# A transformer layer's feed-forward part: Strassen's seven products over both layers instead of Winograd's form over part of the first

## The chip, the cores and the metric

The kernel runs on one core of a Trainium2 chip. Its engines work side by side, each through its own queue in order: TensorE (PE) multiplies, VectorE (DVE) and ScalarE (ACT) work on tiles in the on-chip memory and on the eight banks in which PE sums, GpSimd (POOL) works on on-chip tiles only and issues some DMAs, and SyncE (SP) issues most of them. The metric is the time of one execution in microseconds (us), as the median of several runs. Tiles have 128 partitions; a size such as 128x320 is partitions by columns.

## What is computed

One layer of a hybrid trunk on 640 tokens of width 1024 (128 context tokens, 512 latent ones), in float32: a modulated RMS norm, an input projection, two attention mixers, a gated merge and output projection, and then the part that the change is about, a feed-forward network of inner width 4096, with a final norm:

```python
x = x + g1 * _merge(a_o, b_o, ga, gb, w_br_a, w_br_b, w_out)
h2 = _rmsnorm(x, n2) * (1 + sc2) + sh2
x = x + g2 * (jnp.square(jax.nn.relu(h2 @ w_mlp_in)) @ w_mlp_out)
y = _rmsnorm(x, final_norm_g)
```

Shift, scale and gate (sh2, sc2, g2 and so on) are products of a conditioning vector with the columns of a 1024 x 6144 matrix, one set for context tokens and one for latent ones.

## The kernel before

Features lie on partitions, tokens on columns, so an activation is eight tiles of 128x640. Every product is made in three passes: each operand is split into a high part of reduced precision (hi) and what is left (lo), and PE sums hi·hi, hi·lo and lo·hi in one bank. The unit of work is one 128-column tile of a weight by one half of the tokens (320): 8 feature tiles deep, 24 matmuls of 128x320 (`gemm_k`, L339 to L341).

A weight tile is loaded (512 KB, SP's queue, tile `wst`), ACT copies its hi part, and DVE or POOL subtracts that to get the lo part (L301, L302); a table names the tiles whose lo part POOL makes. Six tiles of hi and lo parts are there in all, so that the preparation runs three weights ahead. `Weights.conv` does this in the order in which `w_order` lists the weights.

The program goes through the input projection with the first norm, attention with the rest of the projection between its steps, the merge (`AOS` on, L1038 and after), the output projection with the second norm, and the feed-forward part. From the merge on, DVE's instructions stand in the order in which they are written; the other engines' order, and DVE's in other places, is set by a scheduler of the framework. Modulation columns that are needed late are computed on DVE from the merge on (`late_mods`, L992: four multiplies of 128x512 with a running sum for each of 32 tiles of 1024 columns, loaded by POOL's queue as `wmt`), paced by a budget for each product.

The feed-forward part has four chunks of 1024 inner features. For each, the first layer gives eight hidden tiles, relu and square split them into parts (`relu2`), and the second layer multiplies them and adds the gated result to x (`add_gated`, L1100). The first layer of chunk 0 is made plainly, 16 units. In chunks 1 to 3 it takes Winograd's form of a 2x2 product: for each pair of weight tiles, seven products of half the depth and half the tokens (12 matmuls each, L1191 to L1193) instead of eight. The blocks of a weight pair and their sums are prepared in `Weights.block` (sums `sr`, L260, on DVE; hi parts, L280, on ACT; lo parts `wb`, L281, two of seven on POOL); those of the activations are formed once, in `t_pieces`, beside chunk 0. The results are combined on DVE from the banks (L1209). The second layer is plain in all four chunks.

Of the kernel before, what the change touches and what calls it, by code (L numbers as in the profile page):

```python
# [28 lines left out]
WP1 = 4  # L29
# [14 lines left out]
PLAIN = (0,)  # L44
SUMP = ()
BLKP = ('A12', 'A22')
RL = 1
OU = 1800
MG = 2
W2P = 2  # L50
# [7 lines left out]
def trunk_layer(ctx: ExitStack, tc: tile.TileContext, xT, small_in, wmodA, wmodB, tabs, cacheK, cacheV, bias,  # L58
# [10 lines left out]
    pp = ctx.enter_context(tc.tile_pool(name="pp", bufs=1, space=bass.MemoryType.PSUM))  # L69
# [13 lines left out]
    def h_pair(name):  # L83
        return tuple(hp_.tile([P, NT], F32R, tag="h", bufs=16, name=name + x) for x in "hl")

    def o_tile(name, dt=F32):
        return hp_.tile([P, NT], dt, tag="o", bufs=9, name=name)
# [4 lines left out]
    def tt_tile(name):  # L92
        return cur["p"].tile([P, NT], F32R, tag="tt", bufs=12, name=name)
# [16 lines left out]
    def r32(ap):  # L110
        return ap.bitcast(F32)
# [52 lines left out]
    def sq_add(acc, x, f, sl):  # L164
        """sum of squares over the feature tiles but the last, whose squares are returned"""
# [6 lines left out]
    def rstd_half(acc, last, rstd, sl):  # L172
        p, n = ps_t(), sl.stop - sl.start
# [6 lines left out]
    def w_order():  # L180
# [10 lines left out]
        for c in range(4):  # L191
            if c in PLAIN:
                for n in range(KT):
                    yield ("w1", 8 * c + n), w1[8 * c + n]
            else:
                for i in range(8 * c, 8 * c + KT, 2):
                    yield ("A11", i), (w1[i], w1[i + 1])
                    for x in ("A12", "S2", "S3", "A22", "S1", "S4"):
                        yield (x, i), None
            for n in range(KT):  # L200
                yield ("w2", 8 * c + n), w2[c, n]
# [5 lines left out]
    def flush_later(todo=None):  # L207
        todo = later if todo is None else todo
        n = len(todo)
        for f in todo[:n]:  # L210
            f()
# [1160 lines left out]
```

## Time and profile before

| | us |
|---|---|
| runs: 1008.04, 1005.4, 1005.79; median | 1005.79 |
| span of the profiled execution, first to last instruction | 1001.3 |
| merge | 349 to 488 |
| output projection and second norm | 488 to 545 |
| feed-forward part, to its last matmul | 545 to 991 |
| last norm and stores | 991 to 1001 |

The profile is of one execution. Its times count from the span's start, and the runs' times hold some us more than the span. Busy times are of each engine; a group's row gives the line in the kernel, engine, operation, tile written and tiles read, shape and count, then busy time in us and the mean of one instruction in ns, then the engine's idle time just before them and whose work ended it. PE's matmuls are pipelined, so a row of it shows 0.31 us for one matmul, though the next starts earlier.

### The profile page before, as it was taken

Reading aid. Unit: us, or ns where it says so; the run is one execution under the profiler, and the core shown is the slowest. Engines: PE = TensorE matmul, PEld = TensorE weight load, DVE = VectorE, ACT = ScalarE, POOL = GpSimd, SP = SyncE. Lnnn points to the kernel's source line nnn. Section 1 sums busy time; section 2 is a strip of 40 time slices with the busy share of each in tenths; the row PEclk is TensorE's granted clock in tenths of the full one; section 3 lists DMA queues with packets and bytes.
Section 4 is the critical chain, followed back from the end, with each engine's and each line's share of the span. In section 5 each row is a group of like instructions: output and inputs, shape, how many; then the busy total and the mean of one; then the engine's idle time right before and its main releaser. Section 6 shows DMA issues by size and latency. Waiting matters only on the chain.

```text
span 1001.3 us, 16554 instructions
## 1 busy us (share of the span) xinstructions
PE 955.0 (95%) x6317; PEld 908.8 (91%) x6317; DVE 705.0 (70%) x1576; ACT 517.6 (52%) x1117; POOL 173.5 (17%) x154
## 2 busy tenths in 40 slices
PE   7979899999899999999999999999999999999996
PEld 5778778978889999999998899999999999999896
DVE  4479898788866789788587677778733884368644
ACT  5475676668655564654324564237611662156542
POOL 0352232212231011201132100012200220012100
PEclk9999899999999999999999899999999999999999
DMA  9942101312543455556742153212320233120302
GB/s 347 208 172 69 31 25 44 77 43 77 135 111 103 133 160 189 181 169 185 224 126 81 47 164 110 85 43 84 106 78 28 85 106 88 60 79 29 126 22 105
DMA packets 34767, 108.47 MB, mean 108 GB/s; under 512 B 4320, under 2 KB 8032, under 8 KB 34688
## 3 DMA queue, kind: packets, MB, share of 16 engines
q1 hardware_dynamic: 27072, 82.63, 26.5%
q0 software_dynamic: 6464, 23.47, 8.1%
q10 hardware_dynamic: 1152, 1.31, 0.4%
q8 instruction: 49, 0.80, 0.3%
q14 instruction: 30, 0.25, 0.1%
HBM read 99.14 MB, written 4.60 MB: 104 GB/s over the span
## 4 chain that ended last, share of the span: by engine, by line
PE 65%; DVE 15%; ACT 8%; issue 3%; DMA 1%; POOL 0%; ACTq 0%; DVEq 0%; POOLq 0%; SPq 0%
PE pg L339 7%; PE pg L340 7%; PE pg L341 7%; PE pss L340 7%; PE pss L341 7%; PE pss L339 6%; PE pt L339 4%; PE pt L341 4%; PE pt L340 4%; DVE sr L260 3%; ACT wb L280 2%; PE pt L653 1%; PE pt L710 1%; DMA wst<-w 1%; DVE n L641 1%
## 5 line engine op out<-in xcount | busy, mean ns | idle before, releaser
L301 ACT ACTIVATE wh<-wst 128x1024 fp32r<-128x1024 f32 x84 | 88.8, 1057 | 112.4 <-PE pg L340 37.9
L302 DVE TENSOR_TENSOR wl<-wst,wh 128x1024 fp32r<-128x1024 f32 x53 | 64.8, 1223 | 67.5 <-ACT wh L301 67.4
L302 POOL TENSOR_TENSOR wl<-wst,wh 128x1024 fp32r<-128x1024 f32 x31 | 75.1, 2423 | 160.0 <-ACT wh L301 151.5
L992 DVE SCALAR_TENSOR_TENSOR mt<-wmt,cb 128x512 f32<-128x512 f32 x128 | 81.4, 686 | 0.0
L281 POOL TENSOR_TENSOR wb<-wst,wb 128x512 fp32r<-128x512 f32 x24 | 31.7, 1322 | 263.4 <-ACT wb L280 226.6
L339 PE MATMUL pss<-hidh,wh 128*128 128x320 f32 x216 | 67.0, 310 | 0.7 <-ACT hidh L1143 0.7
L340 PE MATMUL pss<-hidl,wh 128*128 128x320 f32 x216 | 67.0, 310 | 0.3
L341 PE MATMUL pss<-hidh,wl 128*128 128x320 f32 x216 | 66.7, 309 | 0.0
L607 DVE TENSOR_TENSOR pl<-pt,ph 128x512 fp32r<-128x512 f32 (+2 forms) x80 | 50.5, 633 | 18.3 <-ACT ph L606 17.3
L606 ACT ACTIVATE ph<-pt 128x512 fp32r<-128x512 f32 (+2 forms) x80 | 44.2, 555 | 28.8 <-PE pt L710 11.7
L280 ACT ACTIVATE wb<-sr 128x512 fp32r<-128x512 f32 x48 | 29.8, 627 | 51.5 <-DVE sr L260 35.6
L1150 DVE TENSOR_TENSOR hidl<-rl,hidh 128x320 fp32r<-128x320 f32 x64 | 37.5, 586 | 25.2 <-ACT hidh L1143 24.6
L988 POOL DMA_DIRECT2D wmt<-wmodB x32 | 17.1, 536 | 174.6 <-DVE mt L992 108.0
L340 PE MATMUL pg<-hidl,wh 128*128 128x320 f32 x144 | 44.7, 310 | 2.2 <-DVE hidl L1150 2.2
L281 DVE TENSOR_TENSOR wb<-sr,wb 128x512 fp32r<-128x512 f32 x48 | 36.0, 755 | 14.2 <-ACT wb L280 14.1
L339 PE MATMUL pg<-hidh,wh 128*128 128x320 f32 x144 | 44.7, 310 | 0.0
L341 PE MATMUL pg<-hidh,wl 128*128 128x320 f32 x144 | 44.5, 309 | 0.0
L340 PE MATMUL pt<-hidl,wh 128*128 128x320 f32 x136 | 42.1, 310 | 1.1 <-DVE hidl L1150 1.1
L341 PE MATMUL pt<-hidh,wl 128*128 128x320 f32 x136 | 42.0, 309 | 0.0
L339 PE MATMUL pt<-hidh,wh 128*128 128x320 f32 x136 | 42.0, 309 | 0.0
L644 ACT ACTIVATE pa<-pss,nm 128x320 f32<-128x320 f32 x64 | 33.1, 522 | 17.2 <-DVE nm L642 17.0
L339 PEld LDWEIGHTS pss<-hidh,wh 128*128 128x128 f32 x216 | 40.5, 188 | 1.5 <-ACT hidh L1143 1.5
(957 smaller groups left out, 3469.9 us busy)
## 6 DMA issues: line engine op xcount, KB each, us to landing
wst<-w SPq DMA_DIRECT2D x64, 512.0 KB, 3.6
wmt<-wmodB POOLq DMA_DIRECT2D x32, 512.0 KB, 4.2
wst<-w_in SPq DMA_DIRECT2D x31, 512.0 KB, 3.6
ms<-wmodA SPq DMA_DIRECT2D x16, 512.0 KB, 8.8
x<-xT SPq DMA_DIRECT2D x16, 320.0 KB, 6.1
bt<-bias SPq DMA_DIRECT2D x16, 320.0 KB, 3.3
wst<-w_br SPq DMA_DIRECT2D x8, 512.0 KB, 4.4
wst<-w_out SPq DMA_DIRECT2D x8, 512.0 KB, 3.5
```

Of the source, the lines that this page charges most:

```text
L280: ACT.activation(t[:, lo4], src, AF.Copy)
L281: later.append(lambda: (nc.gpsimd if name in BLKP else DVE).tensor_sub(t[:, hi4], src, r32(t[:, lo4])))
L301: ACT.activation(hi, st, AF.Copy)
L302: (nc.gpsimd if key in WPOOLSET else DVE).tensor_sub(lo, st, r32(hi))
L339: PE.matmul(ps, wh[:, k], xh[:, sl], start=first, stop=False)
L340: PE.matmul(ps, wh[:, k], xl[:, sl], start=False, stop=False)
L341: PE.matmul(ps, wl[:, k], xh[:, sl], start=False, stop=last)
L606: ACT.activation(ph[:, :n], pt[:, :n], AF.Copy)
L607: DVE.tensor_sub(pl[:, :n], pt[:, :n], r32(ph[:, :n]))
L644: ACT.activation(p[:, HALVES[j]], ps[j][:, :HT], AF.Exp, bias=nm, accum_out=s2[:, j:j + 1])
L992: DVE.scalar_tensor_tensor(t, st[:, q * 512:(q + 1) * 512], 1.0, r32(cb[2 * q + i][:, :512]), op0=OP.mult, op1=OP.mult, accum_out=parts[:, ...
L1150: DVE.tensor_sub(dst[1][:, sl], r[:, :HT], r32(dst[0][:, sl]))
```

## The change

Both layers of the feed-forward part are made by Strassen's form with 7 products of half the depth and half the tokens for each pair of weight tiles, 16 pairs in each layer. The operand blocks are A11 to A22 of a weight pair and B11 to B22 of the activations (feature halves by token halves). Each of the seven products M1 to M7 goes over all the pairs in turn, so that its activation operand is formed and split once (`make_set`, `form`), and its weight operand for each pair. The hidden layer of 4096 features stays on chip in float32 (`HID`), and the second layer sums its depth of four chunks in one bank for each product and pair. The products come in groups: in layer 1 M2 and M4, then M1, M6 and M7, then M3 and M5; in layer 2 M2 and M4, M3 and M5, M1 and M6, and M7.

A weight pair's blocks are loaded again for each group that needs them. POOL forms every sum of weight blocks (L1163) and, for the products in `POOL_LOW`, the lo part (L1180); DVE makes the other lo parts. There are four tiles each for `s` and `s2`, in which sums wait, six for loads, and six for split operands as before. The gates of the feed-forward part (tiles 24 to 31 of the modulation) go from DVE to POOL, with ACT summing (`last_mods`), in the merge. DVE's written order now ends with the output projection; after it the scheduler sets all. The eight banks of the feed-forward part are one pool.

```diff
+POOL_LOW = {(1, "M4"), (2, "M4"), (2, "M3")}
...
+    def last_mods(n):
+        st = dp.tile([P, 1024], F32, tag="ms2", bufs=1, name="wmg")
+        MISC.dma_start(st, wmodB[n])
+        for q in range(2):
+            for i in range(2):
+                t = wp.tile([P, 512], F32, tag="s", bufs=4, name="mg")
+                nc.gpsimd.tensor_mul(t, st[:, q * 512:(q + 1) * 512], cb[2 * q + i])
+                ACT.activation(t, t, AF.Copy, accum_out=parts[:, q, n, i:i + 1])
...
+    def split_set(t, src):
+        ACT.activation(t[:, 0:4], src, AF.Copy)
+        DVE.tensor_sub(t[:, 4:8], src, r32(t[:, 0:4]))
+        return t
+
+    def form(raw, name):
+        a, b, op = {"D4": (B21, B11, OP.subtract), "D3": (B12, B22, OP.subtract), "M1": (B11, B22, OP.add),
+                    "M7": (B21, B11, OP.add), "M6": (B11, B12, OP.add)}[name]
+        DVE.tensor_tensor(raw[a], raw[a], raw[b], op=op)
...
+            if names[0] == "M2":
+                self.loads.append((k, [(whole, b)]))
+                self.spec[st, n, "M2"] = ((k, 0), (k, 1), OP.add)
+                self.spec[st, n, "M4"] = ((k, 1),)
...
+                nc.gpsimd.tensor_tensor(t, self.tiles[k0][:, 4 * h0:4 * h0 + 4], self.tiles[k1][:, 4 * h1:4 * h1 + 4], op=op)
...
+            t = wp.tile([P, KT, P], F32R, tag="w" + "hl"[self.n_conv % 2], bufs=3, name="wb")
+            ACT.activation(t[:, 0:4], src, AF.Copy)
+            (nc.gpsimd if (x[0], x[2]) in POOL_LOW else DVE).tensor_sub(t[:, 4:8], src, r32(t[:, 0:4]))
...
+    def mm(ps, w, x, first, last):
+        wh, wl, xh, xl = w[:, 0:4], w[:, 4:8], x[:, 0:4], x[:, 4:8]
+        for k in range(4):
+            PE.matmul(ps, wh[:, k], xh[:, k], start=first and k == 0, stop=False, skip_group_check=True)
+            PE.matmul(ps, wh[:, k], xl[:, k], start=False, stop=False, skip_group_check=True)
+            PE.matmul(ps, wl[:, k], xh[:, k], start=False, stop=last and k == 3, skip_group_check=True)
...
+        mm(b, w, H2S[o], o not in ("M4", "M7", "M5"), o not in ("M2", "M1", "M3"))
+        if o == "M2":
+            ACT.activation(s22, b, AF.Copy, scale=-1.0)
+        elif o == "M4":
+            DVE.tensor_add(s11, b, s22)
+            relu2(s21, b)
+        elif o in ("M1", "M6"):
+            DVE.tensor_add(s22, s22, b)
+        elif o == "M7":
+            DVE.tensor_add(s11, s11, b)
+        elif o == "M3":
+            DVE.tensor_add(s22, s22, b)
+            DVE.tensor_add(s11, s11, b)
+            DVE.scalar_tensor_tensor(s22, s22, 0.0, s22, op0=OP.max, op1=OP.mult)
+        else:
+            relu2(s12, b)
+            DVE.tensor_sub(s11, s11, b)
+            relu2(s11, s11)
...
+    def layer2(n, o, w, x):
+        c, j = n // 4, n % 4
+        if c == 0:
+            PS[2, j, o] = bank()
+        b = PS[2, j, o]
+        mm(b, w, x, c == 0, c == 3)
+        if c < 3:
+            return
+        for i, h, minus in TO[o]:
+            f = 2 * j + i
+            off = HALVES[h].start
+            for sl, g in SEGS[h]:
+                gate = (neg[:, f] if minus else mod(3, f))[:, g:g + 1]
+                DVE.scalar_tensor_tensor(X1[f][:, sl], b[:, sl.start - off:sl.stop - off], gate, X1[f][:, sl],
+                                         op0=OP.mult, op1=OP.add)
...
+            if o == "M2" and j == 2:
+                form(HID[c], "D3")
+                form(HID[c], "M1")
+                form(HID[c], "M7")
```

How it moves instructions, at three places. The first is POOL's queue in a Winograd chunk before, where a lo part (`wb`) is followed by the next:

```order
L281 TENSOR_TENSOR wb_7728<-wst_7655,wb_7728 128x512
L281 TENSOR_TENSOR wb_7867<-wst2_7657,wb_7867 128x512
L281 TENSOR_TENSOR wb_7951<-wst_7722,wb_7951 128x512
L281 TENSOR_TENSOR wb_8013<-wst2_7724,wb_8013 128x512
L281 TENSOR_TENSOR wb_8106<-wst_7926,wb_8106 128x512
```

and now in layer 2's M2 and M4, where each pair has a sum (`ws`) and a lo part:

```order
L1163 TENSOR_TENSOR ws_9101<-wst_9099 128x512
L1180 TENSOR_TENSOR wb_9175<-wst2_8886,wb_9175 128x512
L1163 TENSOR_TENSOR ws2_9144<-wst2_9142 128x512
L1180 TENSOR_TENSOR wb_9214<-wst_8929,wb_9214 128x512
L1163 TENSOR_TENSOR ws_9180<-wst2_9178 128x512
L1180 TENSOR_TENSOR wb_9250<-wst2_9012,wb_9250 128x512
```

Before, POOL has two instructions for seven products here; now it has two for every two. The second place is DVE's queue. Before, in a Winograd chunk, sums of weight blocks (`sr`), lo parts and adds from the banks (`pt`, `pss`, `pg`) follow each other:

```order
L281 TENSOR_TENSOR wb_7930<-wst_7722,wb_7930 128x512
L1209 TENSOR_TENSOR pv_7888<-pv_7888,pt_7938 128x320
L260 TENSOR_TENSOR sr_7968<-wst2_7724 128x512
L260 TENSOR_TENSOR sr_7970<-sr_7968,wst_7722 128x512
L1209 TENSOR_TENSOR cc_7889<-pv_7888,pss_7955 128x320
L281 TENSOR_TENSOR wb_7972<-sr_7970,wb_7972 128x512
```

and now, at the same place as POOL's rows above, sums (`hid`, `s12`) and lo parts (`set`) of whole activation blocks stand between the lo parts of the weights:

```order
L1046 TENSOR_TENSOR setM4_9276<-hid_6749,setM4_9276 128x1280
L1180 TENSOR_TENSOR wb_9269<-ws2_9057,wb_9269 128x512
L1053 TENSOR_TENSOR s12_8803<-s12_8803,hid_6748 128x1280
L1053 TENSOR_TENSOR hid_6750<-hid_6750,hid_6748 128x1280
L1180 TENSOR_TENSOR wb_9310<-ws_9101,wb_9310 128x512
L1053 TENSOR_TENSOR hid_6749<-hid_6749,hid_6750 128x1280
L1053 TENSOR_TENSOR s12_8972<-s12_8972,hid_6745 128x1280
L1180 TENSOR_TENSOR wb_9344<-ws2_9144,wb_9344 128x512
```

A lo part of a weight there has up to two instructions of 1280 columns ahead of it. The third place is POOL's queue in the merge, which held loads of modulation columns (`wmt`) and now holds multiplies (`mg`) among them:

```order
L908 TENSOR_TENSOR mg_4638<-wmg_4633,cb_4358 128x512
L908 TENSOR_TENSOR mg_4641<-wmg_4633,cb_4359 128x512
L908 TENSOR_TENSOR mg_4644<-wmg_4633,cb_4360 128x512
L915 DMA wmt_4678<-wmodB 128x1024
L904 DMA wmg_4881<-wmodB 128x1024
L915 DMA wmt_4717<-wmodB 128x1024
L908 TENSOR_TENSOR mg_4883<-wmg_4881,cb_4357 128x512
```

A load of `wmt` now stands behind the multiplies that are ahead of it in the queue.

More of the change, by code (lines that the diff above doesn't have):

```diff
@@ L289, in conv @@
+            self.st, self.t = {}, {}
+            self.nd = self.nc = self.live = 0
+            self.after = lambda: None
+        def feed(self):
+            while self.nd < len(self.order) and len(self.st) < 2:
+                key, src = self.order[self.nd]
+                self.st[key] = wp.tile([P, KT, P], F32, tag="st", bufs=2, name="wst")
+                nc.sync.dma_start(self.st[key], src.rearrange("p (k n) -> p k n", k=KT))
+                self.nd += 1
         def conv(self):
```

552 lines of the change are left out of this document (289 added, 263 removed).

## The prediction

> **What bounds the kernel now.** I read the page's busy shares first, then a table by stage, then the idle gaps of TensorE (PE), then VectorE (DVE) and GpSimd (POOL) beside each other in time.
>
> ```profile
> PE 955.0 (95%) x6317; PEld 908.8 (91%) x6317; DVE 705.0 (70%) x1576; ACT 517.6 (52%) x1117; POOL 173.5 (17%) x154
> ```
>
> The table gives for each stretch its length, then each engine's busy time and instruction count, then PE's granted clock. In order: the merge; the output projection; the MLP's first inner chunk; the first Winograd chunk; the second layer on it and on the next chunk; the last second layer; the tail.
>
> ```profile
> 349.00:487.60 138.60, 138.60 (x945) 138.28 (x944) 113.01 (x284) 72.31 (x140) 18.09 (x34) 1.00 0.57 178
> 487.60:545.00 57.40, 57.40 (x390) 57.08 (x389) 41.06 (x97) 19.56 (x36) 14.27 (x9) 1.00 0.42 137
> 545.00:609.90 64.90, 60.58 (x390) 59.38 (x389) 45.07 (x95) 35.74 (x71) 8.77 (x6) 0.95 0.32 98
> 666.20:715.50 49.30, 49.30 (x338) 49.28 (x337) 41.69 (x68) 32.24 (x68) 11.72 (x8) 1.00 0.27 86
> 715.50:774.20 58.70, 57.25 (x386) 56.36 (x385) 24.51 (x44) 13.99 (x21) 3.69 (x2) 1.00 0.23 73
> 823.50:882.10 58.60, 57.16 (x386) 56.43 (x385) 24.42 (x44) 13.88 (x21) 3.69 (x2) 1.00 0.23 72
> 931.50:991.60 60.10, 58.65 (x391) 57.37 (x390) 29.41 (x58) 27.84 (x49) 2.39 (x1) 1.00 0.23 76
> 991.60:1001.30 9.70, 1.33 (x4) 0.31 (x3) 3.86 (x9) 2.03 (x4) 0.00 (x0) 0.82 0.37 135
> ```
>
> The last matmul of the MLP, in PE's order in time:
>
> ```profile
> 991.27 0.31 PE L341 MATMUL pss<-hidh,wl 128*128 128x320 f32 x1
> ```
>
> From 349 us on PE hardly stops. In the merge 945 matmuls take 138.60 us, 0.1467 us each, the price of a 128x320 matmul that follows another. The MLP's matmuls run from 545.0 to 991.4 us, 446.4 us; 8.7 of these are idle (4.3 at the start, 1.45 at each later second layer). DVE and ScalarE (ACT) have slack beside it. So PE sets the pace, and a kernel with fewer matmuls is faster as long as the others keep up.
>
> **What the others cost together** is where I put most weight. First POOL at two places, then DVE at the same two:
>
> ```profile
> 678.92 1.30 POOL L281 TENSOR_TENSOR wb<-wst,wb 128x512 fp32r<-128x512 f32 x1 [3.86 <-ACT wb L280]
> 709.59 2.42 POOL L302 TENSOR_TENSOR wl<-wst,wh 128x1024 fp32r<-128x1024 f32 x1 [5.42 <-ACT wh L301]
> ```
>
> ```profile
> 679.35 0.49 DVE L1209 TENSOR_TENSOR pv<-pv,pt 128x320 f32<-128x320 f32 x1
> 681.63 0.69 DVE L260 TENSOR_TENSOR sr<-wst,sr 128x512 f32<-128x512 f32 x1
> 709.63 2.92 DVE L260 TENSOR_TENSOR sr<-wst,sr 128x512 f32<-128x512 f32 x1
> ```
>
> The same DVE sum of two on-chip tiles takes 0.69 us at 681.63 and 2.92 us at 709.63, where it ends at 712.55, 0.54 us after POOL's instruction (712.01): it stood still until POOL was done. The one at 679.35, which reads a PSUM bank (pt) and one tile, ran at its usual 0.49 us inside POOL's instruction. So a DVE instruction with both inputs on chip and a POOL tensor_tensor exclude each other. Call the thing they share the port, and DVE work with a bank as an input free of it.
>
> [...]
>
> **Prices.** Means from the groups that keep shapes apart, and the range of one tile's instructions:
>
> ```profile
> L281 POOL TENSOR_TENSOR wb<-wst,wb 128x512 fp32r<-128x512 f32 x24 | 31.7, 1322 | 263.4 <-ACT wb L280 226.6 <-DVE x L1100 36.8
> L302 POOL TENSOR_TENSOR wl<-wst,wh 128x1024 fp32r<-128x1024 f32 x31 | 75.1, 2423 | 160.0 <-ACT wh L301 151.5 <-PE pt L653 6.8 <-PE po L660 1.5
> L607 DVE TENSOR_TENSOR pl<-pt,ph 128x512 fp32r<-128x512 f32 x56 | 38.4, 685 | 12.3 <-ACT ph L606 11.5
> L1209 DVE TENSOR_TENSOR cc<-pv,pss 128x320 f32<-128x320 f32 x20 | 9.6, 481 | 0.2
> L1168 DVE TENSOR_TENSOR hr<-hh0h,hh0l x1: 818/818/818, 614.5 to 614.5; 128x640 f32<-128x640 f32 x1
> L1170 DVE TENSOR_TENSOR t<-hr x4: 479/485/485, 615.9 to 656.4; 128x320 f32<-128x320 f32 x4
> L280 ACT ACTIVATE wb<-wst 128x512 fp32r<-128x512 f32 x36 | 22.0, 619 | 26.6 <-PE pss L340 11.8 <-PE pt L340 8.9 <-PE pg L340 6.0
> L1140 ACT ACTIVATE rl<-cd 128x320 f32<-128x320 f32 x24 | 10.9, 454 | 0.0
> L1142 ACT ACTIVATE rl<-rl 128x320 f32<-128x320 f32 x64 | 29.9, 467 | 1.3
> ```
>
> A POOL instruction on 128x512 holds the port for between 1.10 us (what 512 more columns cost, 2.423 less 1.322) and 1.32; I take 1.2, since its start can overlap. A DVE one on 128x512: 0.55 (the 0.54 above) to 0.69, I take 0.6. One on 128x1280 isn't in the trace: 320 more columns cost 0.818 less 0.485, 0.333, so 1.33 to 1.48 (0.818 and twice 0.333); I take 1.4. One on 128x320: 0.35 to 0.49, I take 0.42.
>
> **The change part by part.** *Matmuls.* Before, 384 in the plain chunk, 3 x 336 in the Winograd ones, 4 x 384 in the second layer: 2,928. After, 16 weight pairs x 7 products x 12 in each layer: 2,688. The 240 that go are worth 240 x 0.1467 = 35.2 us. A product is 1.76 us, and what is left is 394 us.
>
> *What feeds them.* Seven groups; per product ACT copies a high part (0.62), and DVE or POOL takes the low part; POOL forms 160 sums (L1163) and 48 low parts (L1180, the table POOL_LOW). DVE does 176 low parts, and on 128x1280 tiles 25 sums (L1053) and 35 low parts (L1046); of 128x320 I count 36 without a bank. The 1280 ones stand in the group where the order puts them.
>
> - A, layer 1, M2 and M4: PE 56.3 us. POOL 32, DVE 16, 1280 6, 320 8: port 38.4 + 9.6 + 8.4 + 3.4 = 59.8.
> - B, layer 1, M1, M6, M7: PE 84.4. POOL 48, DVE 48, 1280 3: 57.6 + 28.8 + 4.2 = 90.6.
> - C, layer 1, M3 and M5: PE 56.3. POOL 16, DVE 32, 1280 9, 320 16: 19.2 + 19.2 + 12.6 + 6.7 = 57.7.
> - D, layer 2, M2 and M4: PE 56.3. POOL 32, DVE 16, 1280 17, 320 3: 38.4 + 9.6 + 23.8 + 1.3 = 73.1.
> - E, layer 2, M3 and M5: PE 56.3. POOL 32, DVE 16, 1280 9, 320 3: 61.9.
> - F, layer 2, M1 and M6: PE 56.3. POOL 32, DVE 32, 1280 11, 320 3: 74.3.
> - G, layer 2, M7: PE 28.1. POOL 16, DVE 16, 1280 2, 320 3: 32.9.
>
> The port asks for more than PE in every group, 450.3 us against 394. At the lower prices, with PE's time where the port asks for less, the groups give 420.4; at the upper ones 497.2. Running ahead can't even this out: sums go at most 8 tiles ahead (two tags of 4 buffers), some 10 us, and no group leaves room. What waits behind it is PE, for a low part that stands in DVE's queue behind the 1280-wide sums.
>
> ACT stays just under: in C it has 16 x (2 x 0.62 + 2 x 0.92) = 49.3 us, with relu and square at 0.45 + 0.47, and about five 1280-wide copies besides. The adds from banks (128 x 320 at 0.48) and the gated sums of layer 2, 72 instead of the MLP's 96 (L1343 against L1100), are free of the port and lie beside POOL's work.
>
> *The start.* The first product waits for the second norm, as now, and for one 1280-wide low part. I keep the 4.3 us of idle; 0 to 10.
>
> *The merge.* The last eight gate columns leave DVE (32 instructions, beside PE in the first inner chunk, where they cost nothing) and become 32 POOL multiplies of 128x512 in the merge: 42 us at 1.32. DVE is busy 113.0 of 138.6 there. If none of it overlaps, 113.0 + 42.2 is 16.6 too much; if the 15 us of DVE that read banks (32 at 0.48) overlap, it just fits. POOL's order has them all in the first half, so I take 4, from 0 to 16. The 24 loads of the other columns stand between them in POOL's queue (its four tiles mg also wait for ACT): a load can start four multiplies, 5.3 us, late.
>
> ```profile
> L992 DVE SCALAR_TENSOR_TENSOR mt<-wmt,cb 128x512 f32<-128x512 f32 x128 | 81.4, 686 | 0.0
> wmt<-wmodB POOLq DMA_DIRECT2D x32, 512.0 KB, 4.2
> ```
>
> DVE uses up a load in 4 x 0.69 us, so two others in hand last 5.5 us; with 4.2 us to land the load can come late by 4, and the next in DVE's queue is a product of the merge, whose bank PE wants back. That lies within the 16.
>
> *Loads.* The merge moved 178 GB/s without a gap on PE. B asks for 1.05 MB in each 5.28 us, 199 GB/s; G for 0.52 MB in 1.76 us, 298 GB/s, for 28 us. The densest stretch of the page moved 347 GB/s (first number of this row):
>
> ```profile
> GB/s 347 208 172 69 31 25 44 77 43 77 135 111 103 133 160 189 181 169 185 224 126 81 47 164 110 85 43 84 106 78 28 85 106 88 60 79 29 126 22 105
> ```
>
> I add 2 us for G, 0 to 5. *The clock.* In the stretch from 545.0 idle of 4.3 us came with a granted clock of 0.95, 3.2 us lost. More idle means more of that, but where PE waits anyway a slower product costs little: 3 us, 0 to 15. *The tail* stays at 9.7 us: half the tokens are normed and stored after the last matmul, as now.
>
> **The sum.** MLP 450.3 + 4.3 = 454.6 against 446.4, +8.2; merge +4, loads +2, clock +3: +17 us on a span of 1001.3. The median of the runs, 1005.79, is 4.5 above this span, for what lies around it; I add the difference to the median: 1023 us. With all lower prices, 420.4 - 446.4 = -26: 980. With all upper ones 497.2 + 10 - 446.4 + 16 + 5 + 15 = +97: 1103.
>
> **The rivals.**
>
> 1. *PE keeps the pace (faster).* POOL's work slips between DVE's, and 394 + 4.3 us replace 446.4: 1005.8 - 48 = 958. For it: the Winograd chunk ran without a gap at DVE 41.69 and POOL 11.72 us of 49.30. Against it: 32 POOL instructions and 17 long DVE ones in D alone ask for 62 us of 56.3. It decides if POOL and DVE together hold the port under 3.52 us for two products. Chance 0.06.
> 2. *The port is the bound, at its lower prices (faster).* Instructions of both engines stand ready, so that every start overlaps: 980 to 1000, middle 988. For it: the 0.54 us. Against it: DVE takes its queue in order and is often at a bank when POOL ends. Chance 0.17.
> 3. *DVE's bank reads don't lie beside POOL's work either.* 112 adds of layer 1 at 0.48, 54 us, and 72 gated sums of some 0.43 us, 31: if half of these 85 comes on top, +42: 1065. For it: in order, DVE reaches a blocked instruction soon and stands there until POOL ends. Chance 0.15.
> 4. *The clock.* If every 4.3 us of idle loses 3.2, 60 us of idle lose some 45, and with half of it hidden in waits that remain, +25: 1048. [...] Chance 0.08.
>
> **How the numbers follow.** My forecast, the port as the bound at middling prices, has 0.54, with 1003 to 1050 as its own range. About 0.3% (3 us) is what a measurement of this kernel tells from no change. Faster: rivals 1 and 2 and a little of the forecast's lower end, 0.24. The same: 0.08, from that lower end. Slower: 0.68. The range, 985 to 1075, leaves out rival 1, the low half of rival 2, and the far end of rival 3.
>
> **What would show it.** Right: PE's busy share falls from 95% to under 90%, its idle time ends with low parts (wb) of DVE and POOL or sums (ws); DVE's 128x512 low parts have a mean well over 0.8 us, with single ones above 1.5; groups D and F take about 72 us each and not 56. Wrong: if PE has no gaps in D and F, the port isn't the bound (rival 1); if DVE's low parts stay at 0.69 us while PE waits, it is another thing, ACT or loads (L1180 would then wait for ACT or for wst).

## The result, and the profile after

The changed kernel takes 1072.95 us (median of 4 runs, 1070.09 to 1075.35) against 1005.6 before: a ratio of 1.067, 95% interval 1.064 to 1.070. The forecast was slower, 1023 us in a range of 985 to 1075: the sign is right, the loss is 67 us and not 17. The profiled execution spans 1068.1 us, 66.8 more than before. Its first page row, and the groups of instructions that feed the products:

```profile
PE 950.1 (89%) x6077; PEld 894.5 (84%) x6077; DVE 869.1 (81%) x1503; ACT 569.0 (53%) x1208; POOL 526.4 (49%) x360
...
L1180 DVE TENSOR_TENSOR wb<-ws,wb 128x512 fp32r<-128x512 f32 x160 | 198.6, 1253 | 21.7 <-ACT wb L1179 19.9
...
L1163 POOL TENSOR_TENSOR ws<-wst 128x512 f32<-128x512 f32 x80 | 135.1, 1695 | 69.8 <-DMA wst<-w 51.9
...
L1163 POOL TENSOR_TENSOR ws<-wst,wst 128x512 f32<-128x512 f32 x80 | 139.4, 1774 | 19.4 <-DMA wst<-w 9.8
```

PE is busy 89% of the time (95% before). DVE's low parts have a mean of 1253 ns; before, one of this shape took 685 (L607).

The table by stage follows. To compare the merge alone, both kernels are read from PE's first matmul on the mixers' outputs (osh) to the first of the output projection. First before:

```profile
360.90:487.60 126.70, 126.70 (x866) 126.70 (x865) 104.00 (x269) 62.33 (x120) 15.96 (x30) 1.00 0.59 185
```

Then after: merge, output projection, and the groups A to G of the prediction:

```profile
359.70:520.20 160.50, 134.98 (x866) 132.48 (x865) 128.06 (x270) 80.64 (x184) 68.82 (x68) 0.94 0.49 163
520.20:577.60 57.40, 57.40 (x390) 57.08 (x389) 37.35 (x74) 20.73 (x39) 16.54 (x9) 1.00 0.40 142
...
577.60:658.80 81.20, 65.11 (x390) 61.70 (x389) 52.84 (x60) 49.41 (x101) 53.75 (x36) 0.90 0.37 129
658.90:743.50 84.60, 84.60 (x578) 84.60 (x578) 84.58 (x98) 33.31 (x52) 80.38 (x48) 1.00 0.53 187
743.50:807.90 64.40, 59.29 (x386) 57.80 (x385) 63.77 (x101) 44.38 (x93) 27.80 (x18) 0.97 0.41 131
807.90:880.30 72.40, 62.53 (x386) 60.95 (x385) 72.33 (x52) 30.27 (x46) 61.33 (x31) 0.93 0.34 108
880.30:949.40 69.10, 60.45 (x386) 59.41 (x385) 60.78 (x62) 35.03 (x53) 58.03 (x35) 0.95 0.40 140
949.40:1017.50 68.10, 60.09 (x386) 57.82 (x385) 66.86 (x55) 28.68 (x43) 58.41 (x31) 0.97 0.63 211
1017.50:1058.00 40.50, 32.72 (x198) 30.54 (x197) 30.97 (x46) 16.42 (x29) 12.25 (x8) 0.87 0.25 79
```

The same 866 matmuls of the merge take 33.8 us more. The MLP (the feed-forward part, groups A to G) takes 480.4 us against 446.4: 34.0 more, with 240 matmuls fewer. The output projection is unchanged. So the loss has two halves of nearly equal size, and the forecast had put 4 us on the first.

The port shows in four records of group A, POOL's first and then DVE's:

```profile
606.32 1.30 POOL L1180 TENSOR_TENSOR wb<-wst,wb 128x512 fp32r<-128x512 f32 x1 [6.32 <-ACT wb L1179]
608.08 2.04 POOL L1180 TENSOR_TENSOR wb<-wst,wb 128x512 fp32r<-128x512 f32 x1 [0.46 <-ACT wb L1179]
```

```profile
604.95 1.49 DVE L1053 TENSOR_TENSOR hr<-hr 128x1280 f32<-128x1280 f32 x1 [1.05 <-ACT hr L1074]
606.36 0.48 DVE L1283 TENSOR_TENSOR hid<-b,hid 128x320 f32<-128x320 f32 x1
606.76 2.21 DVE L1053 TENSOR_TENSOR hr<-hr 128x1280 f32<-128x1280 f32 x1
```

The add from a bank at 606.36 runs inside POOL's instruction at its usual 0.48 us. The 1280-wide sum at 606.76 has to wait until POOL ends at 607.62: 2.21 us in place of 1.49. The next POOL instruction, at 608.08, waits in turn for the end of that sum (608.97) and takes 2.04 in place of 1.30. So POOL's records also hold its waits.

Of the four executions of run e1 below, the one that was profiled had a granted clock of 0.74 and took 1157.5 us, so e1's ratio is that of the other three and it has no row in the table by stage.

### The profile page after: what moved, and what is told of

The parts are those of the page before. It is cut to its first block, busy times and chain, and to the rows that moved or that the text cites. A ratio compares the mean times of both kernels' runs of the same rounds, so it can differ in the third digit from the quotient of the medians.

```text
span 1068.1 us, 16611 instructions
## 1 busy us (share of the span) xinstructions
PE 950.1 (89%) x6077; PEld 894.5 (84%) x6077; DVE 869.1 (81%) x1503; ACT 569.0 (53%) x1208; POOL 526.4 (49%) x360
## 4 chain that ended last, share of the span: by engine, by line
PE 42%; DVE 30%; POOL 9%; issue 7%; DMA 6%; ACT 5%; SPq 0%; DVEq 0%; POOLq 0%; ACTq 0%
DVE wb L1180 11%; PE b L1247 4%; PE pg L254 4%; POOL mg L908 4%; PE b L1245 4%; PE b L1246 4%; PE pg L255 4%; PE pg L256 4%; DVE setM L1046 3%; DMA wmg<-wmodB 2%; POOL ws L1163 2%; PE pss L254 2%; PE pss L255 2%; PE pss L256 2%; DMA wst<-w 2%
## 5 line engine op out<-in xcount | busy, mean ns | idle before, releaser
L1247 PE MATMUL b<-setM,wb 128*128 128x320 f32 x896 | 286.1, 320 | 36.2 <-DVE wb L1180 23.7
L1245 PE MATMUL b<-setM,wb 128*128 128x320 f32 x896 | 285.7, 319 | 12.2 <-DVE hid L1291 3.8
L1246 PE MATMUL b<-setM,wb 128*128 128x320 f32 x896 | 284.0, 317 | 6.2 <-DVE setM L1046 6.2
L1180 DVE TENSOR_TENSOR wb<-ws,wb 128x512 fp32r<-128x512 f32 x160 | 198.6, 1253 | 21.7 <-ACT wb L1179 19.9
L1247 PEld LDWEIGHTS b<-setM,wb 128*128 128x128 f32 x896 | 174.6, 195 | 43.1 <-DVE wb L1180 28.7
L1245 PEld LDWEIGHTS b<-setM,wb 128*128 128x128 f32 x896 | 174.6, 195 | 15.1 <-ACT wb L1179 4.5
L1246 PEld LDWEIGHTS b<-setM,wb 128*128 128x128 f32 x896 | 174.8, 195 | 7.7 <-DVE setM L1046 7.4
L1163 POOL TENSOR_TENSOR ws<-wst 128x512 f32<-128x512 f32 x80 | 135.1, 1695 | 69.8 <-DMA wst<-w 51.9
L1179 ACT ACTIVATE wb<-ws 128x512 fp32r<-128x512 f32 x160 | 99.2, 627 | 128.5 <-PE b L1247 107.0
L1163 POOL TENSOR_TENSOR ws<-wst,wst 128x512 f32<-128x512 f32 x80 | 139.4, 1774 | 19.4 <-DMA wst<-w 9.8
L254 PE MATMUL pg<-h,wh 128*128 128x320 f32 x352 | 112.7, 320 | 1.6 <-ACT raw L729 1.0
L255 PE MATMUL pg<-h,wh 128*128 128x320 f32 x352 | 110.8, 315 | 0.0
L256 PE MATMUL pg<-h,wl 128*128 128x320 f32 x352 | 110.4, 314 | 0.2 <-DVE wl L223 0.2
L1180 POOL TENSOR_TENSOR wb<-wst,wb 128x512 fp32r<-128x512 f32 x48 | 86.4, 1805 | 42.6 <-ACT wb L1179 42.6
L919 DVE SCALAR_TENSOR_TENSOR mt<-wmt,cb 128x512 f32<-128x512 f32 x96 | 82.4, 859 | 3.4 <-DMA wmt<-wmodB 1.0
L254 PEld LDWEIGHTS pg<-h,wh 128*128 128x128 f32 x352 | 67.2, 191 | 5.7 <-ACT raw L729 3.4
L255 PEld LDWEIGHTS pg<-h,wh 128*128 128x128 f32 x352 | 67.0, 190 | 1.5 <-issue 0.2
L256 PEld LDWEIGHTS pg<-h,wl 128*128 128x128 f32 x352 | 67.0, 190 | 1.2 <-DVE wl L223 0.5
L523 DVE TENSOR_TENSOR pl<-pt,ph 128x512 fp32r<-128x512 f32 (+2 forms) x80 | 50.5, 632 | 16.8 <-ACT ph L522 15.8
```

The costliest lines, as they stand in the source:

```text
L254: PE.matmul(ps, wh[:, k], xh[:, sl], start=first, stop=False)
L255: PE.matmul(ps, wh[:, k], xl[:, sl], start=False, stop=False)
L256: PE.matmul(ps, wl[:, k], xh[:, sl], start=False, stop=last)
L919: DVE.scalar_tensor_tensor(t, st[:, q * 512:(q + 1) * 512], 1.0, cb[2 * q + i], op0=OP.mult, op1=OP.mult, accum_out=parts[:, q, n, i:i + 1])
L1163: nc.gpsimd.tensor_tensor(t, self.tiles[k0][:, 4 * h0:4 * h0 + 4], self.tiles[k1][:, 4 * h1:4 * h1 + 4], op=op)
L1179: ACT.activation(t[:, 0:4], src, AF.Copy)
```

## The experiments

All times by stage, from the same table for each run's profiled execution; "out" is the output projection, A to G are as in the prediction. The last column is the median of the runs (one run where no ratio is given below).

| | merge | out | A | B | C | D | E | F | G | whole |
|---|---|---|---|---|---|---|---|---|---|---|
| changed kernel | 160.5 | 57.4 | 81.2 | 84.6 | 64.4 | 72.4 | 69.1 | 68.1 | 40.5 | 1073.0 |
| e2 | 165.3 | 57.4 | 81.9 | 84.5 | 66.7 | 73.8 | 66.1 | 69.6 | 41.9 | 1079.9 |
| e3 | 161.6 | 57.4 | 81.5 | 86.1 | 65.3 | 66.3 | 61.7 | 72.3 | 41.9 | 1067.4 |
| e4 | 161.7 | 57.4 | 69.2 | 84.5 | 57.5 | 60.3 | 56.3 | 56.3 | 29.2 | 1003.9 |
| e5 | 137.2 | 71.4 | 79.8 | 84.5 | 63.6 | 73.5 | 66.4 | 69.4 | 41.8 | 1062.3 |
| e6 | 163.2 | 57.4 | 80.0 | 84.5 | 66.8 | 74.0 | 64.7 | 69.6 | 41.1 | 1072.8 |
| e7 | 137.8 | 70.5 | 81.3 | 86.2 | 69.4 | 66.3 | 61.3 | 71.9 | 41.9 | 1055.6 |
| e8 | 137.1 | 71.1 | 81.3 | 86.0 | 66.8 | 62.2 | 63.5 | 69.1 | 37.2 | 1047.6 |
| e9 | 145.7 | 57.4 | 80.8 | 84.4 | 67.7 | 73.7 | 65.0 | 69.2 | 40.9 | 1056.6 |
| e10 | 151.3 | 57.4 | 84.1 | 84.5 | 65.2 | 73.5 | 66.4 | 69.4 | 41.6 | 1069.1 |
| e11 | 164.1 | 57.4 | 79.7 | 84.5 | 65.5 | 74.1 | 64.5 | 69.4 | 36.7 | 1071.9 |
| e12 | 136.4 | 71.1 | 68.7 | 88.2 | 67.2 | 59.6 | 64.8 | 63.5 | 35.9 | 1028.6 |
| e13 | 153.3 | 65.7 | 80.9 | 84.5 | 66.4 | 74.4 | 65.2 | 69.5 | 41.3 | 1075.8 |
| e14 | 146.2 | 67.9 | 79.9 | 84.5 | 67.2 | 74.1 | 64.4 | 69.5 | 41.2 | 1066.8 |
| e15 | 148.4 | 66.1 | 69.5 | 88.1 | 67.1 | 59.4 | 64.1 | 64.0 | 35.9 | 1037.5 |
| e16 | 126.7 | 57.4 | 80.2 | 84.5 | 67.2 | 73.4 | 67.4 | 68.4 | 41.8 | 1038.5 |
| e17 | 126.8 | 57.4 | 79.9 | 84.5 | 63.8 | 73.4 | 66.1 | 69.4 | 41.9 | 1033.7 |

The stages scatter from run to run even where nothing in them is changed. In the runs that leave the MLP as it is (the changed kernel, e2, e5, e6, e9, e10, e13, e14, e16, e17), A takes 79.8 to 84.1, C 63.6 to 67.7, D 72.4 to 74.4, E 64.4 to 69.1, F 68.1 to 69.6 and G 40.5 to 41.9; in those that leave the merge as it is (the changed kernel, e3, e4, e11), the merge takes 160.5 to 164.1. Differences within these are not read.

**The sums on POOL (e4).** Each product that needs a sum of two weight blocks takes one of them in its place, so the result is that of other weights; loads, copies, low parts and matmuls stay.

```diff
+            self.spec = {x: (ops[0],) for x, ops in self.spec.items()}
-            self.sums = [x for x in self.spec if len(self.spec[x]) == 3]
+            self.sums = []
```

> POOL's 160 sums of weight blocks are left out: each product takes one block in place of the sum of two, with the same loads, copies, low parts and matmuls. The output is that of other weights. Port theory: 160 x 1.2 = 192 us of the port go; the groups fall to PE's pace: M1+M6+M7 84, M2+M4 of layer 2 about 57, M3+M5 57, M1+M6 57 to 60, M7 30 to 35; M3+M5 of layer 1 stays at 62 to 64, since DVE alone has that much there; the MLP takes 415 to 430 us against 480.5 and the whole about 1010. Rival (ACT, the loads or the order of the queues hold PE, not POOL's sums): the MLP stays above 455.

```profile
732.40:789.90 57.50, 56.91 (x385) 56.29 (x385) 54.20 (x99) 44.29 (x93) 2.92 (x2) 1.00 0.48 149
789.90:850.20 60.30, 57.17 (x387) 56.38 (x386) 60.23 (x54) 31.55 (x49) 25.89 (x16) 1.00 0.40 131
850.20:906.50 56.30, 56.30 (x386) 56.30 (x386) 41.82 (x59) 33.47 (x50) 23.06 (x14) 1.00 0.46 146
906.50:962.80 56.30, 56.30 (x386) 56.30 (x385) 46.36 (x69) 33.08 (x50) 0.00 (x0) 1.00 0.79 248
```

These are C to F. The MLP takes 413.3 us, 67 less than with the sums and 33 less than before the change. E and F run without a gap on PE; D has 3 us of gaps, with DVE busy throughout. So the matmuls that the change saves are worth what was expected, and POOL's sums take all of it back and as much again. F moved 248 GB/s without a gap, so there the loads are not the cause. C fell to 57.5, where 62 to 64 was expected: DVE is not too slow by itself there (54.2 us busy), it loses time to POOL.

**The low parts on DVE (e3).**

```diff
-POOL_LOW = {(1, "M4"), (2, "M4"), (2, "M3")}
+POOL_LOW = set()
```

> The 48 low parts that POOL forms go to DVE; nothing else. Port theory: a low part costs the port 1.2 us on POOL and 0.6 on DVE, 16 of them each in the groups M2+M4 of layer 1, M2+M4 and M3+M5 of layer 2; the two of layer 2 were 98% and 94% port, so each gets 9.6 us shorter: 72.4 to about 63, 69.1 to about 60; the first, which had 16 us of other idle, gains 5 to 10. In all about 24 to 29 us, 1046. Rival (DVE's own time is the bound, POOL's exclusion is not): DVE, busy 72.33 of 72.4 us in M2+M4 of layer 2, gets 16 x 0.69 = 11 us more there: 83 us, and the whole is slower, about 1095.

```profile
813.10:879.40 66.30, 59.25 (x386) 56.34 (x385) 66.30 (x63) 30.07 (x46) 24.62 (x15) 1.00 0.36 113
```

This is D with 16 more instructions on DVE: 6 us shorter where the rival expected 11 longer. E falls by 3 to 7. So in D the port decides and not DVE's own time; the gain is smaller than the 9.6 that the prices gave. A does not move at all, and F gets some 3 us longer, for which the runs show no reason. The ratio to before is 1.062 (1.056 to 1.068).

**The gate columns on DVE (e1, e5).** The edit of both is shown here. Both also pace the columns faster: OU is 1000 in place of 1800, and MCOST is 1500 in e1 and 1300 in e5, in place of 1600. In e5 they end before the second norm:

```diff
-    MODS = [*range(8), *(8 * i + f for f in range(KT) for i in (1, 2))]
+    MODS = [*range(8), *(8 * i + f for f in range(KT) for i in (1, 2)), *range(24, 32)]
-        last_mods(24 + n)
+    mod_step(64 - lm_n[0])      # at the end of the output projection
```

> Undoes one part of the change: the last eight gate columns go back from POOL (with ACT's running sums) to DVE, now spread over the merge and the output projection; the seven products stay. Both theories of the merge's loss (171.2 us against 138.6 before) put it down to these eight columns and expect the merge at 138 to 143 us, the output projection near 57.4, and the whole 27 to 33 us below 1073, about 1043. If the merge stays above 165, the loss has another cause (the new places of the tiles, the loads). The MLP is expected unchanged at 480 us by all.

> As the first run with the gate columns on DVE, but their multiplies end before the second norm, so that none stands in DVE's queue at the MLP's start. If the first one's small gain (8 us where 30 were expected) came from its multiplies at the MLP's start: merge 138 to 145, output projection 57.4, M2+M4 of layer 1 at 81 or less, the whole 1038 to 1046. If the merge itself did not get shorter by it, the merge stays above 160 and the whole near 1065; then neither POOL's multiplies nor the running sums were its cause.

e1 took 1066.2 us, ratio 1.060 (1.055 to 1.064); e5 1062.3, ratio 1.058 (1.054 to 1.062). In e5 the merge falls by 23 us, and the output projection grows by 14: there PE waits up to 9.5 us for DVE's sum of squares (L173), whose adds stand behind gate columns. Neither expectation had this. Before the change these columns lay in the MLP's first chunk, where DVE had time to spare. Of the groups that now stand ahead of layer 2, B and C have DVE busy almost throughout; A leaves it idle for 28 us, but no run puts all the columns there.

**What in POOL's columns costs the merge.** In the changed kernel the waits from 360 to 470 us show a chain (engine, what waited, for whom; total, times, longest):

```profile
ACT mg L909 <- POOL mg L908: 39.3, 22, 5.0
DVE ml L1000 <- ACT mh L999: 25.9, 10, 8.3
...
PE pg L256 <- DVE wl L223: 10.4, 2, 10.2
```

ACT's running sums wait for POOL, and the products' own work stands behind them in ACT's queue, then in DVE's, until PE waits for a weight. Three runs try to cut it: e2 without the running sums, e6 with other loads out of POOL's queue, e10 with the columns in two half buffers.

```diff
-                ACT.activation(t, t, AF.Copy, accum_out=parts[:, q, n, i:i + 1])      # e2
-            MISC.dma_start(st, wmodB[n])                        # e6, in late_mods
+            nc.sync.dma_start(st, wmodB[n])
-                    MISC.dma_start(s[:, :HT], spill...)         # e6, the stored gates
+                    nc.sync.dma_start(s[:, :HT], spill...)
+            st = dp.tile([P, 512], F32, tag="ms2", bufs=2, name="wmg")               # e10, with e6
+            nc.sync.dma_start(st, wmodB[n][:, q * 512:(q + 1) * 512])
```

> POOL's 32 multiplies for the last eight gate columns stay in the merge, with their loads; ACT's 32 copies with a running sum behind them are left out, so these gates are zero. Queue theory: PE stopped because the copies stood at the head of ACT's queue and waited for POOL (39.3 us in all); without them ACT's work for the products is in time and the merge takes 140 to 148 us. Port theory: POOL's 32 multiplies (1.57 us each in the record) and DVE's 96 with both inputs on chip still exclude each other, and the merge stays at 160 to 171.

> POOL's 32 multiplies and ACT's running sums stay in the merge; the loads that stood between them in POOL's queue (DVE's gate columns and the four stored gate tiles) are issued from SyncE's queue. Theory of POOL's queue: without the running sums ACT waited up to 28.5 us for a stored gate tile, whose load stood behind multiplies in POOL's queue; with those loads elsewhere the merge takes 142 to 155 us and the whole gets 10 to 25 us shorter. Port theory (multiplies on POOL and DVE exclude each other): merge stays at 160 to 171, and the whole at 1065 to 1075.

> All work stays. The gate columns that POOL multiplies are loaded by halves into two buffers, and all gate columns and stored gate tiles from SyncE's queue. Chain theory: a load now lies beside the multiplies of the half before, a column takes 5.5 to 7 us in place of 10, and eight of them 45 to 56 us in place of 80; ACT's waits for POOL get shorter and the merge comes to 143 to 153 us. Port theory: the multiplies come closer together, so DVE is held more in that time; the merge stays at 158 or gets longer.

e2 is no better (165.3), and with it fell the theory that I had made from these waits, that ACT's queue was the cause. Its own waits show what took the place:

```profile
ACT sg L950 <- DMA sg<-gate: 30.6, 2, 28.5
...
PE pg L254 <- DVE sg L997: 13.9, 1, 13.9
```

The loads of the stored gates are issued from POOL's queue, behind the multiplies; ACT's sigmoid now waits for them. e6 takes these loads away and leaves the running sums: 163.2. e10 shortens the chain itself and gets 9 us. Then e9 takes both ways out of POOL's chain away (its gates, like e2's, are left at zero):

> The edits of e2 and e6 together: ACT's running sums of the last eight gate columns are left out (these gates are zero), and DVE's gate columns and the stored gate tiles are loaded from SyncE's queue. POOL's 32 multiplies stay, beside DVE's 96. Chain theory: one column takes POOL some 10 us (4 us for the load into its single buffer, 5 to 6 for four multiplies), and whatever stands behind this chain is late: with e2 it was the stored gate tiles in POOL's queue, with e6 ACT's queue behind the running sums; with both gone the merge takes 137 to 145 us. Port theory: the multiplies exclude DVE as before, and the merge stays at 158 to 171.

It takes 145.7: 15 us less than the changed kernel, 19 more than before. Spreading POOL's multiplies over the whole merge (POOL in program order, e13; also without the running sums, e14) does not help:

```diff
-    manual.enter_context(tc.manual_schedule(engines={DVE.engine}))
+    manual.enter_context(tc.manual_schedule(engines={DVE.engine, nc.gpsimd.engine}))
```

> POOL takes its instructions in the order of the program in the merge and the output projection, in place of an order that the scheduler chooses: four multiplies after each of the eight outputs, with the loads of DVE's gate columns between them, so that they spread over the merge. All work stays. Times of the merge from its first matmul on the mixers' outputs to the first of the output projection (126.7 us before, 160.5 after). Port in the first half: in the first 108 us DVE had 90.8 us of work before, and 42 us of POOL's are 25 too much there; spread over the whole merge 113 and 42 are 16 too much at most, so 128 to 145. Chain theory: ACT's running sums still wait for POOL, and the merge stays above 150.

> As the run before, and ACT's running sums of these columns left out (these gates are zero). If both causes count and nothing else does, the merge (same stretch) takes 127 to 138 us. If it is no shorter than in the run before, the running sums cost nothing once the multiplies are spread. If it stays above 145, a third cause is there.

Merge and output projection come to 219.0 and 214.1 together, against 217.9: what the merge gains the next stage loses. In program order POOL's queue waits for DVE (28.7 us in e13 and 28.4 in e14, for DVE to free a gate column's buffer), and ACT waits for POOL longer (52.4 us in e13). e16 and e17 leave the eight columns out altogether, with the queues of the changed kernel and with those of e9:

> The last eight gate columns are left out on every engine (these gates are zero); the queues are as in the changed kernel. If the columns are the whole cause, the merge (first matmul on the mixers' outputs to the first of the output projection: 126.7 us before, 160.5 after) takes 126 to 130 us and the output projection 57.4. If it stays above 135, a third cause is there (the places of the tiles, the order of the queues).

> As the run before, with DVE's other gate columns and the stored gate tiles loaded from SyncE's queue, as in e9, which had 145.8 us. Port theory: nothing in e9 waits for POOL's multiplies, so they cost only by holding DVE, 32 x 0.4 to 0.6 us and what DVE's queue makes of it: this run takes 126 to 132 us, and the 14 to 20 us between the two are the port. Rival (moving the loads costs it): this run takes 138 to 146.

The merges of e16, e17 and e9:

```profile
359.00:485.70 126.70, 126.70 (x866) 126.70 (x865) 110.64 (x273) 61.80 (x120) 15.43 (x29) 1.00 0.55 183
```

```profile
358.60:485.40 126.80, 126.80 (x867) 126.80 (x866) 109.32 (x269) 62.72 (x120) 0.00 (x0) 1.00 0.58 181
```

```profile
359.80:505.50 145.70, 131.85 (x865) 129.76 (x865) 131.56 (x267) 60.66 (x119) 56.44 (x39) 0.98 0.55 178
```

Without the columns the merge is at 126.7 again, so they are the whole cause, and moving the loads costs nothing by itself. e9 and e17 differ only in the columns' loads and POOL's 32 multiplies, and no other engine's work waits for these: 18.9 us, of which 13.9 are gaps on PE and 5 are slower matmuls. I take this as the port, 0.6 us a multiply (18.9 over 32, an estimate): DVE is busy 22 us longer for the same instructions, and of its 85 gate multiplies (L919) in e9's merge the 24 that lie beside one of POOL's have a mean of 1.38 us, the other 61 one of 0.69. The other 14.8 us of the 33.8 are what e9 takes away, the chain of waits; since the merge scatters from 160.5 to 164.1, this share is known to some 4 us only.

**The start and the last group (e11).**

```diff
-  seq(16, ("M2", "M4"), 1)
+  seq(16, ("M2", "M4"), 2)        # layer 1
-  [(4 * c + n, "M7") for n in range(4) for c in range(4)]
+  [(4 * c + n, "M7") for c2 in (0, 2) for n in (0, 1) for c in (c2, c2 + 1)] + [(4 * c + n, "M7") for n in (2, 3) for c in range(4)]
-            while self.n_conv < len(self.todo) and W.live < 6:
+            while self.n_conv < len(self.todo) and W.live < 6 and self.ready():
```

The last lines, which e12 and e15 have too, let a weight be prepared ahead only when its block is loaded or its sum formed; what they do alone was not run.

> Two orders of products: M4 of layer 1 follows M2 at a distance of two pairs in place of one, and M7 of layer 2 takes the inner chunks 0 and 1 of two outputs before the chunks 2 and 3. Start theory: in M2+M4 of layer 1 (81.2 us) 7 us of idle come from low parts that stand in DVE's queue behind the 1280-wide operands of M4, and 8 us from the slower clock after such gaps; with M4 later the group takes 70 to 76. Of M7's 40.5 us, 7.7 are idle, nearly all for the sets of chunks 2 and 3; with 7 us of products ahead of them the group takes 32 to 36. Rival (port): M2+M4 and M7 stay within 2 us, since the same work holds the port.

PE's gaps in A, of the changed kernel, in order of time:

```profile
583.50 0.42 PE L1245 MATMUL b<-setM,wb 128*128 128x320 f32 x1 [2.20 <-ACT wb L1179]
588.80 0.63 PE L1247 MATMUL b<-setM,wb 128*128 128x320 f32 x1 [4.75 <-DVE wb L1180]
...
615.17 0.41 PE L1247 MATMUL b<-setM,wb 128*128 128x320 f32 x1 [2.11 <-POOL wb L1180]
...
652.91 0.64 PE L1247 MATMUL b<-setM,wb 128*128 128x320 f32 x1 [4.66 <-POOL wb L1180]
```

and of e11:

```profile
597.72 0.60 PE L1250 MATMUL b<-setM,wb 128*128 128x320 f32 x1 [7.74 <-DVE x L1031]
...
659.57 0.63 PE L1252 MATMUL b<-setM,wb 128*128 128x320 f32 x1 [6.73 <-POOL wb L1180]
```

G falls to 36.7, a little short of the 32 to 36 expected, as the wait for the sets of the later chunks goes. A stays: its first gap moves to the output projection's last adds on DVE (L1031), and those at POOL's low parts are still there.

**Together (e7, e8, e12, e15).** e7 is e5 with e3. e8 adds every second sum of layer 2 on DVE. e12 adds all sums of M1+M6 on DVE and the two orders of e11. e15 is e12 with the gate columns on POOL in program order, as in e13.

```diff
-                nc.gpsimd.tensor_tensor(t, ...)
+                (DVE if x[0] == 2 and self.n_sum % 2 else nc.gpsimd).tensor_tensor(t, ...)      # e8
```

> The two parts together: gate columns on DVE before the second norm, and all low parts on DVE. If they add up: e3 gave 12 to 14 us in M2+M4 and M3+M5 of layer 2 and lost 4 in M1+M6, in all 6; with the merge at 140 the whole comes to 1030 to 1040. M2+M4 of layer 1 (81 us in all versions with POOL's sums) is the open one: if its loss comes from the loads that wait for POOL's low parts to free a buffer, it falls to 70 to 75 here; if from DVE's queue at the start, it stays at 80.

> As the one before, and every second sum of layer 2 is made by DVE: 40 sums. Port theory: a sum costs the port 1.2 us on POOL and 0.6 on DVE, so M2+M4 gets 4.8, M3+M5 4.8, M1+M6 9.6 us shorter where the port decides: M1+M6 from 72 to 60 to 64, the others to 57 to 61; the whole 10 to 18 us below the kernel before it. Rival (DVE's own time decides): M1+M6, with DVE busy all of its 72.3 us, gets 16 x 0.69 = 11 us longer.

> Gate columns on DVE, all low parts on DVE, half the sums of layer 2 and all of M1+M6's on DVE, and the two orders. Port theory with the start theory: M2+M4 70 to 76, M1+M6 62 to 66, M7 32 to 36, the rest as in e8 (M1+M6+M7 86, M3+M5 66, M2+M4 62, M3+M5 63): MLP 442 to 455 us; merge and output projection 208 as in e8: the whole 1022 to 1035, still above the kernel before. If DVE's own time decides, M1+M6 gets longer than 69 and the whole stays above 1045.

> The MLP of e12 (all low parts on DVE, most sums of layer 2 on DVE, the two orders), with the gate columns on POOL in the spread order in place of DVE. MLP as in e12, 448 us. Merge and output projection, 207.5 there (136.5 and 71.1): if spreading works, 128 to 145 and 57.4, so 185 to 203 and the whole 1006 to 1024; if not, 160 and 57.4, and the whole near 1038.

Ratios to before: e7 1.052 (1.047 to 1.056), e8 1.043 (1.040 to 1.046), e12 1.024 (1.017 to 1.030), e15 1.033 (1.028 to 1.038). e7 and e8 leave A at 81.3, which was the open question of e7: low parts on DVE alone do nothing there. With the later M4 besides, it falls to 68.7 in e12 and, with the gate columns on POOL, to 69.5 in e15. A needs both edits: e3 and e7 with the one and e11 with the other stay at 79.7 to 81.5. In e8 the sums moved to DVE save 4 us in D, 3 in F, 5 in G and nothing in E, where the port's prices gave 4.8 in D and E and 9.6 in F. In F DVE is now busy throughout:

```profile
929.20:998.30 69.10, 60.13 (x385) 56.30 (x385) 69.07 (x86) 30.73 (x46) 26.80 (x16) 1.00 0.64 211
```

In G PE no longer waits for the operand sets of the last chunks, as in e11.

e12's MLP takes 447.9 us, about what the kernel before takes for 240 matmuls more; its gate columns cost the other 23. No version of these beats the kernel before.

## Why the prediction was right and wrong

*What bounds it: right in D and F.* The port was to be the bound, and D and F were to take about 72 us each: 72.4 and 68.1. From the records of each group one can work out in what share of it at least one runs of POOL's instructions and DVE's with no bank as an input: B 99%, D 98%, E 94%, F 100%; A 87%, C 84%, G 68%. In D and F the port explains all of the time. B was forecast at 90.6 by the port, but it ran at PE's own pace, 84.6 us without a gap, so there the port was full and not the bound. The forecasts of B, D and F sum to 238.0 us, measured 225.1: POOL's price of 1.2 was somewhat high. In B the port was held for 83.5 us; less DVE's 48 x 0.6 and 3 x 1.4, 50.5 are left for 48 POOL instructions, 1.05 each, just under the lower bound. A DVE add that reads a bank was free of it, as the prediction had it: 0.48 us at 606.36, inside POOL's instruction.

*The matmul term: right.* With the sums gone the MLP is 33 us shorter than before (e4), against 35.2 in the sum.

*The merge: the step that failed.* "I take 4, from 0 to 16" became 33.8. It went wrong twice. The bound of 16 set POOL's 42 us against DVE's free time over all of the merge, though the step itself said that they all stand in the first half. The kernel before, in that half (the third pair of numbers is DVE's):

```profile
349.00:380.00 31.00, 31.00 (x212) 30.68 (x211) 25.93 (x61) 18.80 (x37) 4.26 (x8) 1.00 0.45 142
380.00:412.00 32.00, 32.00 (x221) 32.00 (x220) 27.54 (x73) 15.87 (x31) 5.63 (x11) 1.00 0.67 223
412.00:457.00 45.00, 45.00 (x309) 45.00 (x309) 37.35 (x97) 24.84 (x50) 5.55 (x11) 1.00 0.52 161
```

DVE is busy 90.8 of these 108 us, and 42 more are 25 too much. The price of the port alone measured 18.9 (e9 less e17). And the step counted late loads against DVE's stock only. It did not ask who else stands behind POOL: ACT's running sums, with the products' work behind them, and the loads of stored gates in POOL's queue. These cost 14.8. Taking either away alone gained nothing (e2, e6); taking both away did (e9).

*The start, and group A: mis-sized.* 4.3 us of idle, 0 to 10, and 59.8 for the group came to 81.2. PE's 390 matmuls at 0.1467 are 57.2; 16.1 are idle, and the other 7.9 are for the most part slower matmuls. The prediction added up each group's port time and took the larger of this and PE's. In A the port had room (87%), and PE waited for the order of the queues: low parts behind the operands of M4 at the start, and POOL's low parts behind its sums later. e12 gives 12.5 of it back, with M4 later and the low parts on DVE.

*C, E and G: mis-sized.* C took 64.4, not 57.7. The port was held for 84% of it, but DVE was busy 63.77: the forecast left its 21.6 us of work from banks out, as free of the port, yet they stand in the same queue. Without POOL's sums DVE was busy 54.2 us there and the group took 57.5 (e4), so the sums add time to a queue that is already nearly full. This fits rival 3's mechanism, in one group of seven: the bank reads are free of the port (over the MLP their 128x320 adds have means of 475 to 483 ns, 481 before), but DVE stands at a blocked instruction ahead of them; only 8.6 of the 21.6 lay beside POOL's work, which there fills 27.8 us, and in B 20.9 of 22.4 did. E was forecast at 61.9 and took 69.1, the top of its scatter (64.4 to 69.1); it reaches the forecast only with the low parts on DVE (61.7 in e3). G, 32.9 and 2 for loads, took 40.5: 7.8 idle, nearly all for the operand sets of the last chunks; none of PE's gaps there ends with a load.

*The clock: larger than its 3 us, and in part hidden.* PE's busy time above 0.1467 us a matmul is 27 us in the MLP (424.8 for 2,710) and 8 in the merge; some 5 of these are the recorded ends of the last matmuls ahead of gaps, and by the starts of the matmuls the slower pace comes to 23 and 7. In D, where the port decides, the slower products are hidden: it has some 5 us of them and took what the port alone gave. So it does not add up with the rest, as the step said; how much of the 30 us shows in the time, no run separates. Rival 4 reckoned 45 us lost for 60 us of idle; it was 30 for 81.

*The sum.* Too little was forecast by 29.8 us in the merge (33.8 less 4), 17.1 in A with its start, 6.7 in C, 7.2 in E and 5.6 in G with its loads, 66.4 in all; too much by 12.9 in B, D and F and by 3 for the clock; what lies before the merge and after the last product, with rounding, takes 0.9 off. That makes 49.6, the distance from +17.2 (+17 in the prediction) to +66.8. The merge is the largest part of it.

## What to carry to other kernels

Where two engines exclude each other, add up their times for each stretch in which the work really stands, not for the whole stage, and count both engines' records as possibly stretched by the other (here 2.21 us in place of 1.49 on DVE, 2.04 in place of 1.30 on POOL). Work that moves to an idle engine also moves into that engine's queue: list all that is issued there, its loads too, and whatever waits for it, before calling it free; where two chains lead from it to the bound, as here, cutting one of them shows nothing. Fewer matmuls pay only if the sums that they need have a place: here the 240 matmuls were worth 33 us and their 160 sums on POOL cost 67.

## What was not expected of the hardware

In the changed kernel PE had a slow phase after a gap of only 1.79 us, and another that began some time after the restart from a wait of 3.81 us:

```profile
842.27 0.41 PE L1247 MATMUL b<-setM,wb 128*128 128x320 f32 x1 [3.81 <-DVE wb L1180]
842.52 0.31 PE L1245 MATMUL b<-setM,wb 128*128 128x320 f32 x1
...
843.64 0.47 PE L1246 MATMUL b<-setM,wb 128*128 128x320 f32 x1
843.91 0.47 PE L1247 MATMUL b<-setM,wb 128*128 128x320 f32 x1
```

Seven matmuls follow at 0.147 us, and then some twelve at 0.267, until 846.6. After the wait of 1.79 us at 853.43 the slow pace came at once, for 13 matmuls; after that of 2.11 at 615.17 it did not come. The granted clock in this trace explains it better than the single gap does. Its records there hold only 1 and 0.5, and their stretches are 3.41 us or whole multiples of that, but for the last, with which they end; the two slow phases are such stretches, from 843.40 and from 853.64. In the 3.41 us before them PE was busy for 1.13 and 1.63 us (33% and 48%). From 330 us to the end of the MLP, every stretch of 3.41 us in which PE was busy for less than 46% was followed by one at half clock, and no stretch at full clock with PE busy for more than 52% was. Between the two both came. So it was the idle time within such a stretch that counted here, not the length of a gap: the wait of 3.81 us lies in two stretches, with 1.53 and 2.29 us of it, that of 2.11 in two with 1.65 and 0.47, that of 1.79 in one; from 768.30, ahead of a stretch at half clock, there were two gaps of 0.22 and 1.44 us. The slower matmuls of the merge and the MLP come to 30 of 1068.1 us, 3%.
